# A two-layer fp32 encoder: the first loads of layer 0, two seams of the FFN-out products and the last norm reordered

## The chip, the cores and the metric

The kernel runs on one core of a Trainium2 chip (trn2). The metric is device time in microseconds (us) of one execution. Engines are named as in the profile: PE (TensorE, matmuls), PEld (its weight loads), DVE (VectorE), ACT (ScalarE), POOL (GpSimd), SP (SyncE, which issues most transfers).

## The reference

Input: `x` (1 x 1024 tokens x 1024), `mem` (256 x 1024), positions, and weights for two layers. Cut to what matters, each layer computes

```
h   = rmsnorm(x, g_pre_mix);  z = h @ w_in          # 1024 -> 256 + 512 + 128 + 128 + 256
y_f = fourier(z_f, w_fourier)                        # FFT over tokens and channels, then 64x64 mixes
y_a = window attention(z_q, z_k, z_v, sink)          # 8 query heads, 2 kv heads, window 128, rope
y_m = memory attention(z_m, rmsnorm(mem, g_mem) @ w_mem_kv)
x   = x + rmsnorm(concat(groupnorms of y) @ w_out, g_post_mix)
h   = rmsnorm(x, g_pre_ffn);  gate, up = split(h @ w_ffn_in)   # 1024 -> 2 x 2816
x   = x + rmsnorm((silu(gate) * up) @ w_ffn_out, g_post_ffn)   # 2816 -> 1024
```

all in float32. The output is `x`.

## The kernel before, in words

**Arithmetic.** Every fp32 operand of a large product is held as two fp32r halves: `hi` is a cast (`split`, L176, on ACT) and `lo` is the difference to the original (L177, on DVE, or POOL where `lo_eng` says so). A product is three matmuls per step, hi·hi, hi·lo, lo·hi (`Acc`, L187). `ffn_in` and `ffn_out` are seven half-size products each (a Strassen scheme): `ffn_in` forms sums of weight blocks, `ffn_out` sums of weight blocks and of activations, which were written to DRAM (`actd`) in their seven combinations.

**Memory.** Two arenas in SBUF are handed out by hand: `at(k, ...)` is unit k (256 columns) of the fp32 or the fp32r arena, a `Ring` goes round a list of such places. Weights are first loaded as raw fp32 into the ring `raws` (three places of 512 columns: 0, 2, 4), then split. A buffer's next load waits until the last reader of its former content is done.

**Order.** The program states the work in an order; the tile framework then plans, with a simulated timeline, in which order each engine and each queue runs its instructions, and adds the semaphore waits. `weave` interleaves streams in the program, `tc.issue_after` holds an instruction behind another one. So what stands early in the program can run late and the other way round, but on the chip each engine's queue has a fixed order.

**Start of layer 0 (L1433 to L1444).** `start_load(t)` loads a 512 KB tile of x into place 32 + 4(t mod 5); `start_tile(t)` computes the token's scale from its squares (`token_scale`, L327 to L330), transposes the tile on PE (`norm_T`, L341), and splits it (L176, L177). `mix.zf_load()` (`load_w`, L383) loads the 256 Fourier columns of `w_in` in four transfers, multiplies them with g_pre_mix on POOL (`scaled`, L369), casts on ACT and forms `lo` on POOL. `mix.zf(half)` multiplies them with 512 tokens at a time (`zT`, L187), then the two small `pq` products. `fourier_tables` makes small tables (`w_fourier`, L535; `abp`, L538), `prep` the sine tables on DVE (L283, L288) and ACT. `mem.make()` loads `mem` and `g_mem`, loads `w_mem_kv` (eight transfers of 256 KB, L383), norms and transposes `mem` (`mTp`, L470) and forms keys and values of the memory (`kmp`, `vmp`, L187). Then come tiles 4 to 7 woven with `zf(0)`, and in the loop `zf(1, 2)`, which is the second half in two parts of 256 tokens, and `kvz_load` (`load_w512`, L399, eight transfers through `raws`).

**`ffn_out` (L1342 to L1408).** For each of the seven products i in the order 5, 3, 4, 1, 7, 2, 6 it goes over n = 11 steps k. `out_sums` loads an actd block and one or two `w_ffn_out` blocks, adds or subtracts the latter (L1338, DVE), splits both into a buffer of the ring `abs_` (6 places in layer 0, 15 in layer 1). Then four row parts p take three matmuls each (`step`, L1357), into four PSUM banks `pts`. After the last k each part is evicted (L1380 to L1399). Products 3 and 7 go on accumulating in the banks of 5 and 1: their matmuls of part p wait until part p of the former product has been evicted. In product 6 of the last layer parts 2 and 3 run after parts 0 and 1, each over all k.

**End of layer 1.** `last_tile` calls `residual_out` (L347 to L356) for each finished tile of 128 tokens: squares of the row of f (ACT, L350), their mean and its power -1/2 on POOL (L235, L237), then for each half of 512 columns f·r·g (L354) and x + f (L355), and the store (L356).

Of the kernel before, what the change touches and what calls it, by code (L numbers as in the profile page):

```python
# [12 lines left out]
F32R = mybir.dt.float32r  # L13
I32 = mybir.dt.int32
BF16 = mybir.dt.bfloat16
# [54 lines left out]
def tile_encoder(ctx: ExitStack, tc: tile.TileContext, T, C, out):  # L70
# [169 lines left out]
    def gain(row, g):  # L240
        nc.sync.dma_start(g, row.partition_broadcast(P))
        return g
# [104 lines left out]
    def residual_out(x, f, g, dst, t):  # L347

        ss = sm(1, "rss")
        nc.scalar.activation(junks(D // 2).bitcast(BF16), f, AF.Square, accum_out=ss)  # L350
        r = rsqrt_mean(ss, D, 1, "rrs")
        for n in range(2):
            ns = slice(n * 512, n * 512 + 512)
            nc.vector.scalar_tensor_tensor(out=f[:, ns], in0=f[:, ns], scalar=r[:, 0:1], in1=g[:, ns], op0=ALU.mult, op1=ALU.mult)  # L354
            (nc.gpsimd if t in (1, 3) else nc.vector).tensor_tensor(out=x[:, ns], in0=x[:, ns], in1=f[:, ns], op=ALU.add)  # L355
            (nc.sync, nc.scalar)[n].dma_start(dst[:, ns], x[:, ns])  # L356
# [84 lines left out]
    class Memory:  # L441
# [7 lines left out]
        def load_k(self):  # L449
            self.wk = [load_w(self.w, ci * P, P, self.kw + 8 * ci) for ci in range(2)]  # L450

        def load_v(self):
            self.wv = load_w(self.w, MW, MW, self.kw + 16)

        def rows(self):
            self.h = [at(self.kx + 4 + 4 * mt, D) for mt in range(2)]
            for mt in range(2):
                nc.sync.dma_start(self.h[mt], T["mem"][0, mt * P : (mt + 1) * P, :])

        def norm(self, mt):  # L460
            if mt == 0:
                self.g = gain(T["g_mem"][self.l], at(self.kx, D))
                self.mT = [[at(self.kt + 8 * i + 4 * kg, 4, NMEM, dt=F32R) for kg in range(2)] for i in range(2)]
# [13 lines left out]
        def keys(self, ci):  # L477
            pt = ps([NMEM], "kmp", self.tag)
            acc = Acc(pt, NK)
            for k in range(NK):  # L480
                acc.add(self.wk[ci][k][0], self.wk[ci][k][1], self.m(0, k), self.m(1, k))
            nc.scalar.activation(at(self.ks + ci, NMEM), pt, AF.Copy, scale=QK_SCALE)
# [9 lines left out]
        def make(self):  # L492
            self.rows()
            self.load_k()
# [25 lines left out]
    class Mix:  # L520
# [26 lines left out]
        def zf_load(self):  # L547
            self.wzf = load_w(self.win, 0, 256, 64, nc.gpsimd, self.g)

# [792 lines left out]
    def ffn_out(l, actd, load, out, after, half, late):  # L1342
# [16 lines left out]
        for i in (5, 3, 4, 1, 7, 2, 6):  # L1359
# [5 lines left out]
            for k in range(n):  # L1365
                ops.append(out_sums(l, actd, i, k))
                for p in range(whole):
                    step(pts[p], p, ops[k], k == 0, k == n - 1, new)
# [6 lines left out]
            for p in range(4):  # L1375
                pt = pts[p]
                if p >= whole:
                    for k in range(n):
                        step(pt, p, ops[k], k == 0, k == n - 1, new)
                if i == 5:  # L1380
                    nc.scalar.copy(c22[p], pt)
                    nc.scalar.copy(c11[p], pt)  # L1382
                if i == 3:
                    nc.scalar.copy(c12[p], pt)
                    TT(out=c22[p], in0=pt, in1=c22[p], op=sub)
                if i == 4:
# [45 lines left out]
    mix = Mix(0, hT, mem)  # L1432
    start_load(0)  # L1433
    gains_T(gpT, T["g_pre_mix"], at(15, P))
    for t in range(1, 4):
        start_load(t)
    mix.zf_load()
    start_load(4)
# [4 lines left out]
    mem.make()  # L1443
    weave([lambda t=t: start_tile(t) for t in range(4, 8)], [lambda: mix.zf(0)])  # L1444

    for l in range(DEPTH):
        mix.zf(1, 2)
        mix.kvz_load()
        kvz = mix.skewed(mix.kvz, mix.kvz_turn, NT)
        weave(mix.fourier_units(), kvz[:8] + [mix.q_load] + kvz[8:])  # L1450
# [143 lines left out]
```

## Time and profile before

| | us |
|---|---|
| median of 3 runs (2010.7 to 2011.73) | 2010.85 |
| the profiled execution's own time | 2013.01 |
| its span | 2011.2 |
| PE busy in it | 1967.6 (98%) |
| DVE, ACT, POOL busy | 1489.6, 1047.6, 657.2 |
| transfers: 288.56 MB | 143 GB/s over the span |

The span is the time from the first to the last instruction of the profiled execution. A line of a timeline gives start, length, engine, line, operation, output<-input, and in brackets how long the engine had stood idle before and who released it. A line of the chain of work that ended last gives start, length and what the end waited for. A line of a table by windows gives, for each stretch, the busy time of the engines named with the number of instructions (x), then the granted TensorE clock, the share of the DMA engines and GB/s. Matmuls overlap in their pipe, so a busy PE need not run at its full rate; the number of matmuls in a window shows that better.

### The profile page before, as it was taken

To read this page: it belongs to the slowest core of one execution; us is meant where nothing else is said; L and a number is where in the kernel's file an instruction comes from. 1 tells how busy PE (TensorE), PEld (TensorE's weight loads), DVE (VectorE), ACT (ScalarE), POOL (GpSimd) and SP (SyncE) were. 2 spreads that over 40 slices of the span, in tenths; PEclk is the share of its full clock that TensorE was granted. 3 is DMA by queue.
4 is the path that set the end of the run, shared out by engine and by line. 5 is a ranking of instruction groups with operands and counts; after the bars stand their busy time and mean duration, and the time that the engine had idled before them with its cause. 6 is when DMAs were issued, how large, how long until landed. Compare 5 with 4: busy or idle time off the path is not lost.

```text
span 2011.2 us, 28323 instructions
## 1 busy us (share of the span) xinstructions
PE 1967.6 (98%) x9587; PEld 1628.7 (81%) x9587; DVE 1489.6 (74%) x2364; ACT 1047.6 (52%) x2204; POOL 657.2 (33%) x793
## 2 busy tenths in 40 slices
PE   8999999999999999999999999999999999999998
PEld 7877888788888888887888778877888888887886
DVE  5566867888777766678866677679887777778776
ACT  6476877643433334554555678676343333345541
POOL 4345445204334333002423654451134333400021
PEclk9999999999999999999999999999999999999999
DMA  6210323444323224979831113244332332379973
GB/s 214 64 59 27 110 101 127 135 131 136 100 95 121 85 88 157 310 265 322 286 132 45 53 59 116 95 147 126 126 120 95 121 100 95 110 232 330 314 273 116
DMA packets 181889, 288.56 MB, mean 143 GB/s; under 512 B 15560, under 2 KB 81648, under 8 KB 181744
## 3 DMA queue, kind: packets, MB, share of 16 engines
q1 hardware_dynamic: 173680, 267.88, 40.1%
q10 hardware_dynamic: 8064, 18.88, 2.4%
q8 instruction: 75, 1.23, 0.3%
q14 instruction: 70, 0.57, 0.1%
HBM read 220.11 MB, written 66.58 MB: 143 GB/s over the span
## 4 chain that ended last, share of the span: by engine, by line
PE 87%; DVE 3%; DMA 3%; ACT 2%; issue 2%; POOL 2%; SPq 0%; DVEq 0%; POOLq 0%; ACTq 0%
PE fo L1357 18%; PE qy L1193 12%; PE qx L1193 12%; PE qc L1193 11%; PE mo L187 7%; PE qz L1193 6%; PE kvp L187 4%; PE qp L187 4%; PE zT L187 2%; PE sc L793 2%; PE pT L831 2%; PE qa L1193 1%; PE av L844 1%; DMA arena_f<-in_w_ffn_out 1%; DVE arena_r L177 1%
## 5 line engine op out<-in xcount | busy, mean ns | idle before, releaser
L1357 PE MATMUL fo<-arena_r 128*128 128x512 f32 x1512 | 354.6, 391 | 6.6 <-ACT big L1382 4.0
L1357 PEld LDWEIGHTS fo<-arena_r 128*128 128x128 f32 x1512 | 284.0, 188 | 66.2 <-ACT big L1382 4.8
L176 ACT CAST arena_r<-arena_f 128x512 fp32r<-128x512 f32 (+2 forms) x344 | 185.8, 572 | 179.5 <-DMA arena_f<-actd 69.2
L177 DVE TENSOR_TENSOR arena_r<-arena_f,arena_r 128x512 fp32r<-128x512 f32 x262 | 182.3, 727 | 52.0 <-ACT arena_r L176 44.2
L1193 PE MATMUL qc<-arena_r,flex 128*128 128x512 f32 x912 | 220.8, 390 | 0.0
L1183 ACT CAST flex<-arena_f 128x512 fp32r<-128x512 f32 x148 | 91.8, 621 | 232.2 <-PE qy L1193 71.3
L1193 PEld LDWEIGHTS qc<-arena_r,flex 128*128 128x128 f32 x912 | 171.1, 188 | 37.1 <-DVE flex L1125 0.2
L1193 PE MATMUL qy<-arena_r,flex 128*128 128x512 f32 x576 | 139.4, 389 | 0.0
L1183 ACT CAST arena_r<-arena_f 128x512 fp32r<-128x512 f32 x92 | 57.0, 621 | 156.6 <-DVE arena_f L1180 63.7
L1193 PEld LDWEIGHTS qy<-arena_r,flex 128*128 128x128 f32 x576 | 108.0, 188 | 22.6
L1184 DVE TENSOR_TENSOR flex<-arena_f,flex 128x512 fp32r<-128x512 f32 x148 | 108.4, 734 | 22.7 <-ACT flex L1183 22.7
L1227 POOL TENSOR_TENSOR arena_f<-arena_f 128x512 f32<-128x512 f32 x36 | 48.1, 1336 | 231.7 <-ACT arena_f L1198 231.7
L1193 PE MATMUL qx<-arena_r 128*128 128x512 f32 x360 | 119.5, 389 | 0.0
L1193 PE MATMUL qy<-arena_r 128*128 128x512 f32 x480 | 116.4, 389 | 0.0
L1184 DVE TENSOR_TENSOR arena_r<-arena_f,arena_r 128x512 fp32r<-128x512 f32 x92 | 67.7, 736 | 62.6 <-ACT arena_r L1183 60.5
L1193 PE MATMUL qz<-arena_r,flex 128*128 128x512 f32 x320 | 106.8, 395 | 0.0
L1259 POOL TENSOR_TENSOR arena_f<-arena_f,flex 128x512 f32<-128x512 f32 x28 | 45.7, 1632 | 184.9 <-DVE arena_f L1230 114.1
L1193 PEld LDWEIGHTS qy<-arena_r 128*128 128x128 f32 x480 | 90.1, 188 | 18.7
L1234 POOL TENSOR_TENSOR arena_f<-arena_f 128x512 f32<-128x512 f32 x36 | 60.0, 1668 | 126.5 <-DVE arena_f L1233 126.5
L187 PE MATMUL mo<-big,arena_r 128*128 128x512 f32 x384 | 100.4, 398 | 0.5 <-ACT arena_f L1043 0.5
L1193 PE MATMUL qx<-flex,flex 128*128 128x512 f32 x304 | 100.1, 390 | 0.0
L1180 DVE TENSOR_TENSOR arena_f<-arena_f 128x512 f32<-128x512 f32 x90 | 92.5, 1033 | 4.4 <-DMA arena_f<-in_w_ffn_in 2.9
(315 smaller groups left out, 4624.1 us busy)
## 6 DMA issues: line engine op xcount, KB each, us to landing
arena_f<-in_w_ffn_out SPq DMA_DIRECT2D x264, 256.0 KB, 4.7
actd<-arena_f SPq DMA_DIRECT2D x154, 256.0 KB, 3.0
arena_f<-actd SPq DMA_DIRECT2D x154, 256.0 KB, 4.5
arena_f<-in_w_ffn_in SPq DMA_DIRECT2D x46, 512.0 KB, 3.9
big<-in_w_ffn_in SPq DMA_DIRECT2D x40, 512.0 KB, 4.5
arena_f<-in_w_in SPq DMA_DIRECT2D x40, 256.0 KB, 2.9
arena_f<-in_x SPq DMA_DIRECT2D x16, 512.0 KB, 5.3
arena_f<-in_w_out SPq DMA_DIRECT2D x32, 256.0 KB, 2.7
```

What stands on the lines that cost most here:

```text
L176: nc.scalar.copy(hi, src)
L177: return (lo_eng or nc.vector).tensor_tensor(out=lo, in0=src, in1=f32(hi), op=ALU.subtract)
L187: mm(self.dst, a, b, start=self.i == 0, stop=self.i == self.n - 1)
L793: mm(pt, lhs, self.kst[g][i][:, k0 * P : k1 * P], start=i == 0, stop=i == 1)
L1180: nc.vector.tensor_tensor(out=s, in0=x, in1=y, op=op)
L1183: self.cast = nc.scalar.copy(w[:, 0], s)
L1184: self.lo = nc.vector.tensor_tensor(out=w[:, 1], in0=s, in1=f32(w[:, 0]), op=ALU.subtract)
L1193: mm(pt, a, b, start=start and n == 0, stop=n == 11, skip_group_check=not start)
L1227: G(out=self.u2, in0=self.u2, in1=self.p1, op=ALU.add)
L1234: G(out=self.p5, in0=self.p1, in1=self.p5, op=ALU.add)
L1259: (G if i % 2 else nc.vector).tensor_tensor(out=q.act[i], in0=c, in1=g[i], op=ALU.mult)
L1357: mm(pt, ab[:, 0, x, sl], ab[:, 1, y], start=new and first and j == 0, stop=last and j == 2, skip_group_check=not new)
```

## The change

Five things differ.

- `residual_out`: the squares are taken for each half of 512 columns by itself, f is multiplied with g before the scale r is known, and r comes in with the addition of x. POOL adds the mean of the first half's squares to the second's.
- `Memory`: the 256 key columns are loaded as one block of weights (rows of 256 columns) in place of two blocks of 128; the gain row is loaded with the rows of `mem`; in layer 0 these three loads stand ahead of `start_load(4)`.
- Start of layer 0: order x0, gains, x1, `w_in`, x2, x3, `mem`, x4. `raws` has seven places until `kvz_load` has been stated, then again three. Two of the new places (44, 46) lie in tile 3's place of x.
- `zf_load` in layer 0: POOL writes `hi` (raw times gain, rounded) and DVE forms `lo` (raw times gain minus hi), 256 columns at a time, in place of POOL, ACT and POOL. `zf(0)` runs in two parts of 256 tokens.
- `ffn_out`: in products 5 and 1 the last three steps k are run part by part: all three for part 0, then for part 1, and so on, each part's eviction behind it. Product 5 is copied from PSUM once and not twice, and product 3's subtraction reads that copy.

```diff
     def residual_out(x, f, g, dst, t):
-        ss = sm(1, "rss")
-        nc.scalar.activation(junks(D // 2).bitcast(BF16), f, AF.Square, accum_out=ss)
-        r = rsqrt_mean(ss, D, 1, "rrs")
-        for n in range(2):
-            ns = slice(n * 512, n * 512 + 512)
-            nc.vector.scalar_tensor_tensor(out=f[:, ns], in0=f[:, ns], scalar=r[:, 0:1], in1=g[:, ns], op0=ALU.mult, op1=ALU.mult)
-            (nc.gpsimd if t in (1, 3) else nc.vector).tensor_tensor(out=x[:, ns], in0=x[:, ns], in1=f[:, ns], op=ALU.add)
+        ss, v, r = (sm(2, "rss2"), sm(2, "rrsv2"), sm(1, "rrs"))
+        cols = [slice(n * 512, n * 512 + 512) for n in range(2)]
+        for n, ns in enumerate(cols):
+            nc.scalar.activation(junks(256).bitcast(BF16), f[:, ns], AF.Square, accum_out=ss[:, n : n + 1])
+            nc.gpsimd.tensor_scalar(
+                out=v[:, n : n + 1], in0=ss[:, n : n + 1], scalar1=1.0 / D, scalar2=v[:, 0:1] if n else EPS, op0=ALU.mult, op1=ALU.add
+            )
+            nc.vector.tensor_tensor(out=f[:, ns], in0=f[:, ns], in1=g[:, ns], op=ALU.mult)
+        nc.gpsimd.tensor_tensor(out=r, in0=v[:, 1:2], in1=mhalf[:, 0:1], op=ALU.pow)
+        for n, ns in enumerate(cols):
+            nc.vector.scalar_tensor_tensor(out=x[:, ns], in0=f[:, ns], scalar=r[:, 0:1], in1=x[:, ns], op0=ALU.mult, op1=ALU.add)
             (nc.sync, nc.scalar)[n].dma_start(dst[:, ns], x[:, ns])
...
         def load_k(self):
-            self.wk = [load_w(self.w, ci * P, P, self.kw + 8 * ci) for ci in range(2)]
+            self.wk = load_w(self.w, 0, MW, self.kw)
...
         def rows(self):
+            self.g = gain(T["g_mem"][self.l], at(self.kx, D))
             self.h = [at(self.kx + 4 + 4 * mt, D) for mt in range(2)]
...
         def make(self):
-            self.rows()
+            if self.l:
+                self.rows()
             self.load_k()
...
         def zf_load(self):
-            self.wzf = load_w(self.win, 0, 256, 64, nc.gpsimd, self.g)
+            if self.l:
+                self.wzf = load_w(self.win, 0, 256, 64, nc.gpsimd, self.g)
+                return
+            self.wzf = []
+            for k0 in (0, 4):
+                hi, lo = at(64 + 2 * k0, 4, 256, dt=F32R), at(68 + 2 * k0, 4, 256, dt=F32R)
+                for j in (0, 2):
+                    raw = raws(2, 256)
+                    r0 = (k0 + j) * P
+                    nc.sync.dma_start(raw, self.win[r0 : r0 + 2 * P, 0:256].rearrange("(k p) c -> p k c", p=P))
+                    for i in range(2):
+                        g = self.g[:, k0 + j + i : k0 + j + i + 1]
+                        h = hi[:, j + i]
+                        nc.gpsimd.tensor_scalar(out=h, in0=raw[:, i], scalar1=g, scalar2=1.0, op0=ALU.mult, op1=ALU.mult)
+                        nc.vector.scalar_tensor_tensor(
+                            out=lo[:, j + i], in0=raw[:, i], scalar=g, in1=f32(h), op0=ALU.mult, op1=ALU.subtract
+                        )
+                self.wzf += [(hi[:, i], lo[:, i]) for i in range(4)]
...
             for k in range(n):
                 ops.append(out_sums(l, actd, i, k))
-                for p in range(whole):
+                for p in range(whole if i not in (5, 1) or k < n - 3 else 0):
                     step(pts[p], p, ops[k], k == 0, k == n - 1, new)
...
             for p in range(4):
                 pt = pts[p]
-                if p >= whole:
-                    for k in range(n):
-                        step(pt, p, ops[k], k == 0, k == n - 1, new)
+                for k in range(0 if p >= whole else n - 3 if i in (5, 1) else n, n):
+                    step(pt, p, ops[k], k == 0, k == n - 1, new)
                 if i == 5:
-                    nc.scalar.copy(c22[p], pt)
                     nc.scalar.copy(c11[p], pt)
                 if i == 3:
                     nc.scalar.copy(c12[p], pt)
-                    TT(out=c22[p], in0=pt, in1=c22[p], op=sub)
+                    TT(out=c22[p], in0=pt, in1=c11[p], op=sub)
...
     start_load(0)
+    raws.ks = (0, 2, 4, 52, 54, 44, 46)
     gains_T(gpT, T["g_pre_mix"], at(15, P))
-    for t in range(1, 4):
+    start_load(1)
+    mix.zf_load()
+    for t in range(2, 4):
         start_load(t)
-    mix.zf_load()
+    mem.rows()
     start_load(4)
...
-    weave([lambda t=t: start_tile(t) for t in range(4, 8)], [lambda: mix.zf(0)])
+    weave([lambda t=t: start_tile(t) for t in range(4, 8)], [lambda: mix.zf(0, 2)])
...
         mix.kvz_load()
+        raws.ks, raws.i = (0, 2, 4), 0
```

More of the change, by code (lines that the diff above doesn't have):

```diff
@@ L461, in norm @@
             if mt == 0:
-                self.g = gain(T["g_mem"][self.l], at(self.kx, D))
                 self.mT = [[at(self.kt + 8 * i + 4 * kg, 4, NMEM, dt=F32R) for kg in range(2)] for i in range(2)]
@@ L479, in keys @@
             acc = Acc(pt, NK)
+            cs = slice(ci * P, ci * P + P)
             for k in range(NK):
-                acc.add(self.wk[ci][k][0], self.wk[ci][k][1], self.m(0, k), self.m(1, k))
+                acc.add(self.wk[k][0][:, cs], self.wk[k][1][:, cs], self.m(0, k), self.m(1, k))
             nc.scalar.activation(at(self.ks + ci, NMEM), pt, AF.Copy, scale=QK_SCALE)
```

## The prediction

> **What bounds the kernel now.** I read the page first, then the chain of waits in order of time for the start, then tables by windows, and last the timelines of the places that the change touches.
>
> ```profile
> PE 1967.6 (98%) x9587; PEld 1628.7 (81%) x9587; DVE 1489.6 (74%) x2364; ACT 1047.6 (52%) x2204; POOL 657.2 (33%) x793
> ```
>
> PE is the bound over the whole span: of 2011.2 us only 43.6 are idle. The change removes no product, so it can gain only what PE loses: idle time, and time in which it is busy below its rate. The chain shows such time at the start, in four transfers on which the end hung:
>
> ```profile
> 6.03 6.67 DMA arena_f<-in_w_fourier
> ...
> 29.65 2.86 DMA arena_f<-in_w_mem_kv
> ...
> 36.85 3.68 DMA arena_f<-in_w_mem_kv
> ...
> 48.26 2.65 DMA arena_f<-in_w_in
> ...
> 57.16 3.12 PE zT L187 x24
> ```
>
> What PE lost there, and why the transfers were late, is in the waits of PE and of SP's queue:
>
> ```profile
> PE zT L187 <- ACT flex L176: 3.6, 1, 3.6
> PE abp L538 <- DMA arena_f<-in_w_fourier: 2.7, 1, 2.7
> ```
>
> ```profile
> SPq L383 <- DMA arena_f<-in_w_mem_kv: 6.9, 2, 5.5
> SPq L383 <- DVE flex L288: 5.1, 2, 4.9
> ```
>
> SP held loads of L383, `w_mem_kv` and a `w_in`, back for 6.9 + 5.1 = 12.0 us, because with three raw places a load needs an old one's last reader, and that sits on DVE behind the sine work (L288). Two windows show the price on PE:
>
> ```profile
> 10.00:15.00 5.00, 2.33 (x12) 2.20 (x12) 2.52 (x5) 4.70 (x12) 4.53 (x10) 1.00 1.00 331
> ...
> 50.00:55.00 5.00, 1.35 (x11) 1.11 (x10) 1.54 (x3) 3.65 (x8) 4.50 (x5) 0.92 0.65 206
> 55.00:60.00 5.00, 5.00 (x34) 5.00 (x33) 2.90 (x4) 3.15 (x6) 1.35 (x2) 0.74 0.28 90
> ```
>
> After the idle at 50 to 55 the granted clock is 0.74. The second place is `ffn_out` (matmuls of L1357 alone; PE's count is the first x):
>
> ```profile
> 820.00:830.00 10.00, 9.54 (x42) 7.57 (x42) 1.00 0.90 320
> 920.00:930.00 10.00, 9.59 (x43) 7.60 (x41) 1.00 0.84 273
> 930.00:940.00 10.00, 7.43 (x32) 5.93 (x32) 1.00 0.97 350
> 1810.00:1820.00 10.00, 6.59 (x30) 5.11 (x28) 0.94 0.99 340
> 1820.00:1830.00 10.00, 9.91 (x32) 7.96 (x33) 0.72 0.96 335
> 1830.00:1840.00 10.00, 10.00 (x46) 8.29 (x45) 1.00 1.02 368
> ```
>
> 46 in 10 us (0.217 us each) is the full rate. At 1810 to 1830, where product 5 ends and 3 begins in layer 1, 30 of 92 are missing, in part from a clock of 0.72 after the gap. Layer 0 misses 4 at the same seam (820 to 830) and 3 + 14 where 1 passes into 7 (920 to 940).
>
> **The change part by part: the tail.** After the last matmul everything is serial:
>
> ```profile
> 2002.56 0.69 DVE L1397 TENSOR_TENSOR big<-fo,big 128x512 f32<-128x512 f32 x1 [1.98 <-PE fo L1357]
> 2003.35 1.06 ACT L350 ACTIVATE arena_f<-big 128x1024 bf16<-128x1024 f32 x1 [6.33 <-DVE big L1397]
> ...
> 2004.58 0.19 POOL L235 TENSOR_SCALAR rrsv<-rss 128x1 f32<-128x1 f32 x1 [6.65 <-ACT arena_f L350]
> 2004.86 0.55 POOL L237 TENSOR_TENSOR rrs<-rrsv,const 128x1 f32<-128x1 f32 x1
> 2005.44 1.42 DVE L354 SCALAR_TENSOR_TENSOR big<-big,rrs,flex 128x512 f32<-128x512 f32 x2 [2.19 <-POOL rrs L237]
> 2006.77 1.29 DVE L355 TENSOR_TENSOR arena_f<-arena_f,big 128x512 f32<-128x512 f32 x2
> 2008.09 0.34 ACTq L356 DMA_DIRECT2D out<-arena_f  x1
> ```
>
> The left half of f is finished by product 2, so its squares and its product with g lie beside product 6. Behind the last eviction ACT squares 512 columns and not 1024: about half of 1.06, a gain of 0.5 (estimate). The multiplication with g runs on DVE while ACT and POOL work (2003.3 to 2005.4, DVE idle 2.19), so of the four DVE operations after the power two are left: from 2005.44 to 2008.06 was 2.62, two take 1.42, a gain of 1.2. The store behind it stays. Sum 1.7; bounds 1.2 (the square saves nothing) and 2.0. For tiles 1 and 3 the addition moves from POOL to DVE, two operations of 0.65 per tile, beside products in which PE is bound: nothing.
>
> **The seams.** The row parts of product 3 wait for the evictions of product 5. In layer 1 these stood in ACT's queue behind casts that waited for DVE and a transfer:
>
> ```profile
> 1818.45 0.62 ACT L176 CAST arena_r<-arena_f 128x512 fp32r<-128x512 f32 x1 [1.07 <-DVE arena_f L1338]
> ...
> 1819.45 0.59 ACT L1382 COPY big<-fo 128x512 f32<-128x512 f32 x1
> ...
> 1820.09 1.65 PE L1357 MATMUL fo<-arena_r 128*128 128x512 f32 x3 [3.50 <-ACT big L1382]
> ```
>
> Run part by part, the last three steps are 9 matmuls per part, so part 0 is finished 27 x 0.217 = 5.9 us before the product's end, part 1 3.9, part 2 2.0, and each needs one copy, not two. The copy of part 0 then has 5.9 us and more, where the gap was 3.50. The price: the operands of the last step are needed when part 0 reaches it, 30 matmuls (6.5 us) before the end and not 12 (2.6): 3.9 us earlier.
>
> ```profile
> 1807.58 0.62 ACT L176 CAST arena_r<-arena_f 128x512 fp32r<-128x512 f32 x1 [0.42 <-DMA arena_f<-actd]
> 1808.23 0.69 DVE L177 TENSOR_TENSOR arena_r<-arena_f,arena_r 128x512 fp32r<-128x512 f32 x1
> ...
> 1813.71 2.88 PE L1357 MATMUL fo<-arena_r 128*128 128x512 f32 x12
> ```
>
> The last step began at 1813.71; its operands, if I read the ring rightly, were there at 1808.92, 4.8 us earlier. So 0.9 us of margin is left. I take 5.5 of the 30 x 0.217 = 6.5 us; part 3's copy is still at the very end and may cost the rest. Bounds 2.5 (operands 3.9 late) to 6.5. At layer 0's seam of 5 the gain is at most 4 x 0.217 = 0.9; I take 0.5. At its seam of 1:
>
> ```profile
> 931.75 0.68 DVE L1390 TENSOR_TENSOR big<-fo,big 128x512 f32<-128x512 f32 x1
> ...
> 932.57 1.61 PE L1357 MATMUL fo<-arena_r 128*128 128x512 f32 x6 [2.60 <-ACT arena_r L176]
> ```
>
> Eviction (till 932.43) and cast end together: DVE and ACT are late with both. The change spreads the evictions but DVE's work stays; I take 1.0, from -3.9 (operands needed earlier) to 17 x 0.217 = 3.7. Seams together 7.0. That three of the six places of layer 0's ring are held to the end costs nothing as long as the other three feed product 3 for its first 3 x 2.6 us.
>
> **The start.** Of the transfers in the chain the last three are held by `raws`; four more places let them start with the tiles of x. Upper end: 2.86 + 3.68 + 2.65 = 9.2, and the 2.7 of `abp`, 11.9; the idle 3.6 at 54 is the third one's effect and not counted again. Lower end: `mem`, `g_mem` and the fourth `w_in` load, 1.75 MB, may now stand in SP's queue ahead of `w_fourier`; at 331 GB/s (last column, 10 to 15) that delays `abp`, and the tiles queued behind it on PE, by 5.3: -5.3.
>
> Which is nearer? What comes next is ACT: 4.70 of 5 us busy at 10 to 15, 3.65 and 3.15 at 50 to 60. It loses the four casts of `w_in` but must do all others in a shorter time. I take half of the upper end, 6. The weights of `zf` now go through POOL and DVE:
>
> ```profile
> L369 POOL TENSOR_SCALAR arena_f<-arena_f,const 128x256 f32<-128x256 f32 x8 | 3.7, 483 | 0.1
> ...
> L288 DVE SCALAR_TENSOR_TENSOR flex<-flex 128x256 f32<-128x256 f32 x10 | 4.6, 458 | 0.1
> ...
> 44.57 1.46 DVE L407 SCALAR_TENSOR_TENSOR big<-arena_f,const,big 128x512 fp32r<-128x512 f32 x1 [0.26 <-ACT big L406]
> ...
> 47.48 0.75 DVE L407 SCALAR_TENSOR_TENSOR big<-arena_f,const,big 128x512 fp32r<-128x512 f32 x1 [0.32 <-ACT big L406]
> ```
>
> Eight steps of 0.483 and a last 0.458 are 4.3 us from first to last. But L407, the same operation at twice the width, took 1.46 beside a POOL operation and 0.75 alone. Doubled on both engines the chain takes 8.2; the 3.9 come off the start's gain at most. [...] `zf(0)` in halves lets its first part start with two tiles; it costs 96 narrow matmuls at 3.12/24 = 0.130 for 48 wide ones at 3.02/12 = 0.252: 0.4.
>
> ```profile
> 31.20 3.02 PE L187 MATMUL zT<-arena_r 128*128 128x512 f32 x12
> ```
>
> The key weights in one block and the order of their rows move the same bytes by as many instructions: nothing.
>
> **Sum.** 1.7 + 7.0 + 6 - 0.4 = 14.3. The profiled execution took 2013.01 (span 2011.2 and 1.8 around it), 2.2 above the median of the runs; the differences come off the median: 2010.85 - 14.3 = 1996.5.
>
> **The rivals.** (1) The start gains little: POOL and DVE hold each other up as above, and ACT's fixed order keeps what transfers no longer hold. For it: ACT's 4.70 of 5. Start 1.5 and not 6: 2001.
> (2) The seams don't do what the text says: the planner may mix the part order again, or the operands come just in time, so that PE waits before the end what it no longer waits after it. For it: the margin of 0.9. Seams 1 and not 7: 2002.5.
> (3) All of it: start 11.9, seams 6.5 + 0.9 + 3.7: 2010.85 - 1.7 - 11.9 + 0.4 - 11.1 = 1986.5.
> (4) Slower: the need for operands 3.9 us earlier decides. Wherever the last step's operands are ready less than 6.5 us before the product's end, PE stands 3.9 and then runs at 0.72 for 10 us (2.8): 6.7. At all four seams 26.8, against 6.5 + 0.9 + 3.7 lost now: 15.7 more. With the start and the tail 2010.85 + 15.7 - 7.3 = 2019. Against it: 15 places in layer 1, and the margin.
>
> **How the numbers follow.** Forecast 0.50, rival (1) 0.22, (2) 0.12, (3) 0.08, (4) 0.08. A measurement can tell about 0.2% (4 us) from no change: faster means below 2006.8. Rivals (1) and (2) together (start 1.5, seams 1) would give 2007, and the start's lower end in place of the 6 2007.8; I put 0.10 on no change. The range reaches from rival (3) over (1) and (2) to that edge: 1987 to 2007. Faster 0.83, same 0.10, slower 0.07.
>
> **What would show it.** The tail: about 7 us, not 8.7, from the last matmul to the end of the span, with two DVE operations after the power. The seam of layer 1: no gap above 1 us, 44 or more matmuls of L1357 in each 10 us, granted clock 1.00. The start: `w_mem_kv` transfers gone from the chain, SP's waits on L383 below 5 us, `zf`'s second half some 6 us earlier. Wrong if a new gap stands inside the last three steps of products 5 or 1, if `abp` waits longer than 2.7 us, or if PE loses time in stages that the change doesn't touch.

## The result, and the profile after

| | us |
|---|---|
| before, median of 6 runs (2007.76 to 2015.37) | 2011.07 |
| after, median of 6 runs (1995.89 to 2003.06) | 1998.99 |
| after : before, 95% interval | 0.994 (0.9924 to 0.9956) |
| after once more, on another chip, median of 6 runs | 1998.57 |
| its ratio | 0.9926 (0.9899 to 0.9953) |
| profiled execution of after: own time, span | 1995.89, 1994.1 |

The change makes the kernel 12.1 us faster (8.8 to 15.3 by the interval); the forecast was 14.3. The two profiled executions lie 17.1 us apart, more than the medians: the one before was 1.9 above its median, the one after 3.1 below.

The first line of the page of after (busy time, share of the span, instructions):

```profile
PE 1961.6 (98%) x9635; PEld 1625.0 (81%) x9635; DVE 1493.8 (75%) x2378; ACT 1043.0 (52%) x2210; POOL 650.5 (33%) x793
```

PE idles 32.5 us of 1994.1, where it was 43.6 of 2011.2; its busy time is 6.0 less although it runs 48 matmuls more. That is the time in which it was busy below its rate.

**Where the 17.1 us went.** The first column gives a point of the program, by the start of the first or the end of the last matmul of the named output in each trace; the last column what was gained since the point above.

| | before | after | gained |
|---|---|---|---|
| layer 0: end of the last `kvp` | 124.24 | 119.74 | 4.5 |
| first `fo` | 795.58 | 790.96 | 0.1 |
| last `fo` | 1026.69 | 1019.43 | 2.65 |
| layer 1: first `qp` | 1109.63 | 1102.38 | 0.0 |
| last `qp` | 1181.02 | 1171.35 | 2.4 |
| first `fo` | 1786.50 | 1776.89 | -0.1 |
| end of the last `fo` | 2002.52 | 1986.50 | 6.4 |
| end of the span | 2011.22 | 1994.11 | 1.1 |

Four of these are places of the change: the start, the two `ffn_out`, the tail. Nothing was forecast for layer 1's key and query stage, where 2.4 were gained; it comes up at the end.

**The seams.** Table by windows of after, its `fo` matmuls (L1380) alone; columns as before: us, PE and PEld busy (x), granted clock, DMA share, GB/s:

```profile
820.00:830.00 10.00, 10.00 (x46) 8.29 (x45) 1.00 0.83 283
920.00:930.00 10.00, 9.65 (x42) 7.39 (x41) 1.00 1.01 360
930.00:940.00 10.00, 9.80 (x44) 7.80 (x43) 1.00 0.89 290
...
1810.00:1820.00 10.00, 10.00 (x46) 8.29 (x45) 1.00 1.01 353
1820.00:1830.00 10.00, 10.00 (x46) 8.29 (x45) 1.00 1.02 366
```

All 46 are there at the seams of product 5; in layer 1 the windows that held 30 and 32 hold 46 at a clock of 1.00. Where 1 passes into 7, 86 stand in two windows, before 75.

**The start.** The three longest waits of PE in the first 70 us of after, without the 4.6 us for the gains (`ggp`) that both kernels have, then one of SP's queue there:

```profile
PE zT L187 <- DVE arena_r L177: 1.6, 1, 1.6
PE zT L187 <- ACT arena_r L176: 1.3, 2, 0.9
PE hTp L341 <- ACT arena_f L495: 1.0, 1, 1.0
```

```profile
SPq L387 <- DVE flex L177: 3.8, 3, 3.2
```

The waits for `w_fourier` (2.7) and for the cast of late weights (3.6) are gone. SP's longest wait on L387 (before L383) is 3.8 us, where the two longest were 12.0 together. With all smaller waits of this line it is 5.6 us, and it was 17.1. Table by windows of after, whole core (PE, PEld, DVE, ACT, POOL busy):

```profile
30.00:35.00 5.00, 3.16 (x23) 2.51 (x22) 5.00 (x13) 4.49 (x11) 2.33 (x4) 1.00 0.68 211
35.00:40.00 5.00, 5.00 (x44) 5.00 (x43) 4.96 (x10) 3.60 (x6) 1.31 (x3) 1.00 0.63 178
40.00:45.00 5.00, 5.00 (x44) 5.00 (x44) 4.93 (x6) 2.77 (x7) 4.82 (x4) 1.00 0.34 103
45.00:50.00 5.00, 4.03 (x34) 3.79 (x34) 4.11 (x7) 2.74 (x6) 2.59 (x5) 1.00 0.00 0
50.00:55.00 5.00, 4.27 (x33) 3.73 (x33) 2.69 (x5) 4.06 (x8) 0.53 (x3) 1.00 0.26 105
```

The hole of before (50 to 55, 1.35 us busy) has become three shallow ones, and in these windows the clock stays at 1.00. No transfer stands in the chain between 26 and 60 us any more; it runs through DVE, which is busy 14.89 of 15 us from 30 to 45.

**The tail.** Timeline of after, from the last eviction on:

```profile
1986.54 0.69 DVE L1418 TENSOR_TENSOR big<-fo,big 128x512 f32<-128x512 f32 x1 [2.63 <-PE fo L1380]
1987.32 0.63 ACT L352 ACTIVATE arena_f<-big 128x512 bf16<-128x512 f32 x1 [6.00 <-DVE big L1418]
...
1988.08 0.69 DVE L356 TENSOR_TENSOR big<-big,flex 128x512 f32<-128x512 f32 x1 [0.85 <-ACT arena_f L352]
1988.22 0.68 POOL L353 TENSOR_SCALAR rrsv<-rss,rrsv 128x1 f32<-128x1 f32 x1 [4.92 <-ACT arena_f L352]
1988.98 0.55 POOL L357 TENSOR_TENSOR rrs<-rrsv,const 128x1 f32<-128x1 f32 x1
1989.57 1.42 DVE L359 SCALAR_TENSOR_TENSOR arena_f<-big,rrs,arena_f 128x512 f32<-128x512 f32 x2 [0.80 <-POOL rrs L357]
```

From the last matmul to the end it is 7.61 us and not 8.70. The square took 0.63 for 1.06, and two operations follow the power. But POOL's step on one column took 0.68 where its like took 0.19 before: it began 0.14 us after DVE's product of two SBUF operands, which had waited for ACT, because it overwrites the f that ACT reads.

### The profile page after: what moved, and what is told of

It is laid out like the page before. It is cut to its first block, busy times and chain, and to the rows that moved or that the text cites. A ratio compares the mean times of both kernels' runs of the same rounds, so it can differ in the third digit from the quotient of the medians.

```text
span 1994.1 us, 28456 instructions
## 1 busy us (share of the span) xinstructions
PE 1961.6 (98%) x9635; PEld 1625.0 (81%) x9635; DVE 1493.8 (75%) x2378; ACT 1043.0 (52%) x2210; POOL 650.5 (33%) x793
## 4 chain that ended last, share of the span: by engine, by line
PE 88%; DVE 3%; ACT 2%; POOL 2%; issue 2%; DMA 1%; DVEq 0%; POOLq 0%; SPq 0%; ACTq 0%
PE fo L1380 19%; PE qx L1216 12%; PE qy L1216 12%; PE qc L1216 11%; PE mo L187 7%; PE qz L1216 6%; PE kvp L187 4%; PE qp L187 4%; PE sc L816 2%; PE zT L187 2%; PE pT L854 2%; PE qa L1216 1%; PE av L867 1%; DMA arena_f<-in_w_in 1%; PE ms L935 1%
## 5 line engine op out<-in xcount | busy, mean ns | idle before, releaser
L1380 PE MATMUL fo<-arena_r 128*128 128x512 f32 x1512 | 354.0, 390 | 0.6 <-DVE arena_r L177 0.5
L1380 PEld LDWEIGHTS fo<-arena_r 128*128 128x128 f32 x1512 | 283.1, 188 | 59.9 <-DVE arena_r L177 0.9
L177 DVE TENSOR_TENSOR arena_r<-arena_f,arena_r 128x512 fp32r<-128x512 f32 x262 | 178.2, 714 | 42.6 <-ACT arena_r L176 32.5
L1216 PE MATMUL qx<-arena_r 128*128 128x512 f32 x360 | 119.5, 389 | 0.0
L1207 DVE TENSOR_TENSOR arena_r<-arena_f,arena_r 128x512 fp32r<-128x512 f32 x92 | 66.7, 725 | 62.3 <-ACT arena_r L1206 60.2
L1361 DVE TENSOR_TENSOR arena_f<-arena_f 128x512 f32<-128x512 f32 x110 | 81.2, 743 | 20.7 <-DMA arena_f<-in_w_ffn_out 19.9
```

The lines of the kernel that those rows point to most:

```text
L177: return (lo_eng or nc.vector).tensor_tensor(out=lo, in0=src, in1=f32(hi), op=ALU.subtract)
L1207: self.lo = nc.vector.tensor_tensor(out=w[:, 1], in0=s, in1=f32(w[:, 0]), op=ALU.subtract)
L1216: mm(pt, a, b, start=start and n == 0, stop=n == 11, skip_group_check=not start)
L1361: nc.vector.tensor_tensor(out=s, in0=x, in1=y, op=op)
L1380: mm(pt, ab[:, 0, x, sl], ab[:, 1, y], start=new and first and j == 0, stop=last and j == 2, skip_group_check=not new)
```

## The experiments

My theory: each of the three parts gains by itself, the seams by the order of the steps (not by the copy that is saved), the start by places and order of the loads together, until DVE is the bound. Rivals: the saved copy frees ACT and that is all; the raw places alone are the start's gain; ACT bounds the start.

**The tail alone.** The edit is the change's `residual_out` and nothing else.

```diff
     def residual_out(x, f, g, dst, t):
-        nc.scalar.activation(junks(D // 2).bitcast(BF16), f, AF.Square, accum_out=ss)
...
+        for n, ns in enumerate(cols):
+            nc.scalar.activation(junks(256).bitcast(BF16), f[:, ns], AF.Square, accum_out=ss[:, n : n + 1])
...
```

> The kernel before with the new residual_out alone. Theory (the three parts act each at its own place): from the last matmul to the end of the span 7.6 us and not 8.7, as in the changed kernel, and nothing else; the time falls by 1.1 us, 0.05%, which timing can hardly tell. The POOL step behind the last squares takes 0.68 and not 0.19, because DVE multiplies f by g beside it. Rival (the tail gains the 1.7 forecast, and the 0.68 is chance): 7.0 us from the last matmul to the end.

Measured: 2009.46 (12 runs), ratio 0.9992 (0.998 to 1.0004). From the last matmul to the end 7.59 us; POOL's step 0.68 again. The tail's gain is 1.1 us, and no time of the whole kernel could show it.

**The seams alone**: the change's edits in `ffn_out`.

```diff
-                for p in range(whole):
+                for p in range(whole if i not in (5, 1) or k < n - 3 else 0):
...
+                for k in range(0 if p >= whole else n - 3 if i in (5, 1) else n, n):
...
-                    nc.scalar.copy(c22[p], pt)
...
-                    TT(out=c22[p], in0=pt, in1=c22[p], op=sub)
+                    TT(out=c22[p], in0=pt, in1=c11[p], op=sub)
```

> The kernel before with the part-by-part order of the last three steps in products 5 and 1 and the single copy. Theory: about 9 us faster (6.4 at the seam of layer 1, 2.7 in layer 0), 0.45%; no gap over 1 us at the layer 1 seam and clock 1.00 there. Rival (the gain of the changed kernel there came from an earlier start, which shifted transfers against the seam): under 4 us.

Measured: 2005.55 (12 runs), ratio 0.997 (0.9959 to 0.9981), 6.0 us (3.8 to 8.2), less than the 9 expected from the two profiles. All 46 matmuls stand in each window at 820, 1810 and 1820, and PE waits at none of the seams of product 5.

**One copy, old order**: of these edits the last three lines.

```diff
-                    nc.scalar.copy(c22[p], pt)
...
-                    TT(out=c22[p], in0=pt, in1=c22[p], op=sub)
+                    TT(out=c22[p], in0=pt, in1=c11[p], op=sub)
```

> The kernel before with product 5 copied from PSUM once and not twice, the order of the steps as before. Theory (the copies stand behind casts that wait, and only the order lets them out earlier): the gap at the layer 1 seam shrinks by the 0.5 us of one copy, to about 3.0; gain below 2 us, or up to 4 if the shorter gap no longer brings the clock down. Rival (ACT's load is the cause, the order only decoration): most of the 6.4 us.

Measured: 2011.32 (12 runs), ratio 0.9993 (0.9981 to 1.0004). Timeline of PE at layer 1's seam:

```profile
1814.24 2.88 PE L1357 MATMUL fo<-arena_r 128*128 128x512 f32 x12
1818.69 0.96 PE L1357 MATMUL fo<-arena_r 128*128 128x512 f32 x3 [1.57 <-ACT big L1381]
```

The gap is still there, 1.57 us for 3.50; about 3.0 was expected. After it the clock stayed at 1.00 here, and layer 1's `ffn_out` took 211.5 us, where the six kernels with the old order and two copies took 214.1 to 216.0. So in this one profile the single copy gained 3 us at the seam, but the time of the kernel shows no gain clear of the noise.

**New order, two copies**: the rest of the edits.

```diff
-                for p in range(whole):
+                for p in range(whole if i not in (5, 1) or k < n - 3 else 0):
...
+                for k in range(0 if p >= whole else n - 3 if i in (5, 1) else n, n):
```

> The kernel before with the part-by-part order of the last three steps in products 5 and 1, and product 5 still copied from PSUM twice. Theory (the order is the cause, the single copy an extra of under 1 us): 5 to 6.5 us faster, no gap over 1 us at the layer 1 seam. Rival (both are needed, since two copies per part, 1.2 us, stand between casts that wait): under 3 us and a gap of 1 us or more.

Measured: 2004.53 (5 runs), ratio 0.9966 (0.9953 to 0.9979), 6.8 us. Its windows, `fo` matmuls alone:

```profile
1810.00:1820.00 10.00, 10.00 (x45) 8.03 (x44) 1.00 1.00 355
1820.00:1830.00 10.00, 10.00 (x46) 8.29 (x45) 1.00 0.98 332
```

So the order alone brings the seams' gain; with it, the second copy costs nothing that can be seen. The rival, that the saved copy is all, falls. That the copy by itself can shorten the gap stays: the two edits work on the same gap, and their gains don't add up.

**The start alone**: every edit outside `residual_out` and `ffn_out`.

```diff
     start_load(0)
+    raws.ks = (0, 2, 4, 52, 54, 44, 46)
...
+    start_load(1)
+    mix.zf_load()
...
+    mem.rows()
     start_load(4)
...
```

> The kernel before with all edits of the start and the memory block, seams and tail as before. Theory: layer 0's first FFN-out matmul comes 4.6 us earlier, as in the changed kernel, and the time falls by 4 to 5 us, 0.2%. Rival (the gain in layer 1's key and query stage, 2.4 us in the profile of the changed kernel, belongs to the memory block or to the ring's new phase): that stage is 2.4 us shorter here too, and the time falls by 7.

Measured: 2006.07 (12 runs), ratio 0.9973 (0.9961 to 0.9986), 5.4 us (2.8 to 7.8). Layer 1's key and query stage took 69.1 us here (before 71.4), as the rival had it, but the time fell by 5.4 and not by 7. The three parts alone sum to 1.6 + 6.0 + 5.4 = 13.0 us, whole 12.1 and 14.9: within their intervals they add up. Then the start was taken apart.

**Only the seven raw places:**

```diff
     start_load(0)
+    raws.ks = (0, 2, 4, 52, 54, 44, 46)
...
+        raws.ks, raws.i = (0, 2, 4), 0
```

> The kernel before with seven places for raw weights until the key and value weights are loaded, all else as before. Theory (the held-back transfers were the loss at the start, as the prediction put it): 3 to 5 us faster, the first FFN-out matmul of layer 0 some 4 us earlier, the memory weights' transfers gone from the chain. Rival (DVE, busy 5.00 of 5 us from 30 to 45 in the changed kernel, is the next bound, so that transfers alone gain little): under 2 us.

Measured: 2015.16 (12 runs), ratio 1.0024 (1.0014 to 1.0034): slower, where 3 to 5 us of gain were expected.

**The whole start, but three raw places:**

```diff
     start_load(0)
-    raws.ks = (0, 2, 4, 52, 54, 44, 46)
```

The line that sets the ring back to its first place behind `kvz_load` stays.

> All edits of the start and the memory block, but three raw places as before. Theory (the places are the cause): 0 to 2 us faster than the kernel before, against 6 with seven places. Rival (order, two-tile products and the POOL and DVE weights gain by themselves): 4 us or more.

Measured: 2017.06 (12 runs), ratio 1.0024 (1.0013 to 1.0035): slower as well.

**The start, but the first `w_in` weights by POOL, ACT and POOL as before:**

```diff
     def zf_load(self):
-            if self.l:
-                self.wzf = load_w(self.win, 0, 256, 64, nc.gpsimd, self.g)
-                return
...
+            self.wzf = load_w(self.win, 0, 256, 64, nc.gpsimd, self.g)
```

> All edits of the start and the memory block, but the first w_in weights made as before, by POOL, ACT and POOL. Theory (places and order are the cause; POOL and DVE hold each other up in the new way, so it gains little): within 1.5 us of the 6 that all edits gain. Rival (the weights' chain is what the first product waits for): 3 us or less, and the first zT matmul at 12 us or later, not at 9.

Measured: 2009.6 (11 runs), ratio 0.9996 (0.9985 to 1.0006): no difference to before. The first `zT` stands at 10.42 us, in the start alone at 8.93.

All three kernels with a part of the start miss its gain, and with it what was expected. At the start itself they don't: the last `kvp` of layer 0 ends earlier in each. They lose it between there and the first `fo` of layer 0, in code that no edit touches, and a good part of it at 360 to 390 us. Timeline of PE there, first of the kernel before, then of the one with seven raw places:

```profile
364.02 1.06 PE L1118 MATMUL hTp<-const,arena_f 128*128 128x128 f32 x8 [1.22 <-DVE arena_f L321]
...
370.84 2.88 PE L1193 MATMUL qc<-arena_r,flex 128*128 128x512 f32 x12
374.25 0.73 PE L1193 MATMUL qa<-arena_r,flex 128*128 128x512 f32 x2 [0.53 <-ACT flex L1183]
```

```profile
372.64 1.04 PE L1118 MATMUL hTp<-const,arena_f 128*128 128x128 f32 x8
373.43 2.99 PE L1193 MATMUL qc<-arena_r,flex 128*128 128x512 f32 x12
379.06 0.96 PE L1193 MATMUL qa<-arena_r,flex 128*128 128x512 f32 x2 [2.64 <-ACT flex L1183]
```

The order of the instructions differs. Before, eight transposes `hTp` stand ahead of the last 24 matmuls of `mo`, which run while their result is split; here they stand behind them, and PE waits 2.64 us for ACT. The window behind this wait, whole core:

```profile
380.00:390.00 10.00, 10.00 (x44) 8.30 (x43) 8.46 (x12) 4.05 (x8) 1.16 (x3) 0.86 0.33 113
```

In this stretch every kernel of the study has one of the two orders, A (as before) or B. The table gives each one's end of the last `kvp` of layer 0, the time from there to its first `fo`, and the lengths of the two `ffn_out` (first to last `fo`):

| kernel | last `kvp` | order | to first `fo` | `ffn_out` 0 | `ffn_out` 1 |
|---|---|---|---|---|---|
| before | 124.2 | A | 671.3 | 231.1 | 216.0 |
| tail alone | 124.9 | A | 672.9 | 231.5 | 214.1 |
| seams alone | 123.4 | A | 672.9 | 227.7 | 209.6 |
| one copy, old order | 125.7 | A | 672.8 | 230.5 | 211.5 |
| new order, two copies | 125.5 | A | 672.8 | 228.7 | 209.8 |
| start alone | 120.1 | A | 671.8 | 231.9 | 214.4 |
| only seven raw places | 122.9 | B | 678.1 | 229.5 | 214.2 |
| start, three raw places | 122.0 | B | 677.8 | 233.6 | 215.1 |
| start, old weights | 120.2 | B | 676.3 | 233.6 | 214.3 |
| after | 119.7 | A | 671.2 | 228.5 | 209.6 |
| after once more | 117.4 | A | 671.8 | 233.1 | 209.6 |
| after, own place for f*g | 119.5 | A | 673.3 | 228.3 | 209.7 |
| after, preparation late | 123.7 | B | 676.3 | 230.5 | 209.6 |
| after, both | 124.1 | B | 674.1 | 228.0 | 209.8 |

The nine kernels of order A take 671.2 to 673.3 us (mean 672.3) from `kvp` to `fo`, the five of order B 674.1 to 678.1 (mean 676.5): 4.2 us, a little less than what the start gains.

The wait above is not the whole of it. Counted from the last `kvp`, at points where PE has run the same matmuls in both orders, order B is behind by 1.0 us on the mean at 258 us of the kernel before, by 3.0 at 325, by 2.5 at 373, just ahead of this wait, and by 4.2 at the first `fo`. In the kernel with three places the wait is 1.13 us, and all of its loss stands earlier.

By its own rows, each kernel gains at the start (the five kernels with the old start have a mean of 124.8) and loses against order A's mean: places alone 1.9 and 5.8, three places 2.8 and 5.5, old weights 4.6 and 4.0. Measured were 4.8 us slower, 4.8 slower and 0.8 faster. The signs fit; 1 us of the first and 2 of the second stay unexplained, and two profiles of one kernel (after, and after once more) differ by 2.3 us at the last `kvp`. That the order is the cause is read from this table: no run turned the order alone.

**The changed kernel once more**, beside three variants on one chip:

> The changed kernel once more, beside three variants of it on the same chip. If what was seen between the two profiles belongs to the change, its ratio to the kernel before is again about 0.994 (0.9925 to 0.9955), the first zT matmul stands near 9.8 us, the first FFN-out matmul of layer 0 near 791 us (4 to 5 us ahead of the kernel before), 46 matmuls in every 10 us of 1800 to 1830, and the granted clock is 1.00 there. The key/query stage of layer 1 is the open point: both kernels waited 1.7 us there, the one before at a granted clock of 0.66 afterwards, the changed one at 1.00. If that difference is chance, the 2.4 us that the changed kernel gained in this stage can be missing here; if it belongs to the change it is there again.

Measured: 1998.57 (6 runs), ratio 0.9926 (0.9899 to 0.9953). First `zT` at 8.74, last `kvp` 2.3 us earlier again, 46 matmuls in each window at layer 1's seam. The key and query stage of layer 1 again took 69.0 us (before 71.4). In this execution `ffn_out` of layer 0 had two waits of 1.4 us at 1008 to 1012, one of them behind a late `actd` transfer, and took 233.1.

**A place of its own for f*g of the right half:**

```diff
-            nc.vector.tensor_tensor(out=f[:, ns], in0=f[:, ns], in1=g[:, ns], op=ALU.mult)
+            fg.append(at(4, 512) if n else f[:, ns])
+            nc.vector.tensor_tensor(out=fg[n], in0=f[:, ns], in1=g[:, ns], op=ALU.mult)
...
-            nc.vector.scalar_tensor_tensor(out=x[:, ns], in0=f[:, ns], scalar=r[:, 0:1], in1=x[:, ns], op0=ALU.mult, op1=ALU.add)
+            nc.vector.scalar_tensor_tensor(out=x[:, ns], in0=fg[n], scalar=r[:, 0:1], in1=x[:, ns], op0=ALU.mult, op1=ALU.add)
```

> The changed kernel, with the right half of f*g in the last residual written to a buffer of its own, so that VectorE needn't wait for ScalarE to have read f. Theory: at the end of the changed kernel GpSimd's one-column step took 0.68 us instead of 0.19 only because VectorE's product of two SBUF operands (0.69 us, started 0.14 us before it) ran beside it. Then VectorE's product starts beside the ScalarE square instead, it is over when GpSimd begins, the step is back at 0.19 us, and from the last matmul to the end 7.6 us become about 7.1 us: some 0.5 us, ratio to the changed kernel 0.9997, far under what a time can tell; the profile rows decide. Rival: the step is slow because its second scalar operand is a column of SBUF instead of a constant. Then it stays at 0.68 us and the tail stays at 7.6 us.

Measured: 1999.59 (7 runs), ratio to before 0.9933 (0.991 to 0.9956); against the changed kernel no difference. Timeline of its tail:

```profile
1990.47 0.69 DVE L358 TENSOR_TENSOR arena_f<-big,flex 128x512 f32<-128x512 f32 x1
1990.53 0.63 ACT L353 ACTIVATE arena_f<-big 128x512 bf16<-128x512 f32 x1 [6.00 <-DVE big L1420]
...
1991.43 0.27 POOL L354 TENSOR_SCALAR rrsv<-rss,rrsv 128x1 f32<-128x1 f32 x1 [6.12 <-ACT arena_f L353]
1991.78 0.55 POOL L359 TENSOR_TENSOR rrs<-rrsv,const 128x1 f32<-128x1 f32 x1
```

With DVE's product over before POOL begins, the step takes 0.27 us, and the tail 7.17 for 7.61. The theory holds, the rival (the column operand) is left with 0.08 us.

**The preparation of the tables behind the second tiles:**

```diff
     mix.fourier_tables(58)
-    prep()
     mem.make()
     weave([lambda t=t: start_tile(t) for t in range(4, 8)], [lambda: mix.zf(0, 2)])
+    prep()
```

> The changed kernel, with the preparation of the norm gains and of the sine and cosine tables of the positions moved behind the second half of the first token tiles: the same instructions, later in each engine's order. Theory: the start of the changed kernel is bound by VectorE, busy 5.00, 4.96 and 4.93 of 5 us between 30 and 45 us, some 4 to 5 us of it this preparation; moved behind, the first kvp matmuls start 2 to 4 us earlier, VectorE shows gaps between 30 and 45 us, and the span falls by 2 to 4 us (ratio to the changed kernel 0.998 to 0.999) if the later stages keep their order. Rival: the bound at the start is the arrival of the weights or ScalarE; then the milestones of the first 100 us move by under 1 us and the time stays, or is 2 to 4 us longer when the preparation is waited for behind it. A second rival: the start gains and it is given back in the out stage, at 130 to 400 us, where another order of the PE's groups leaves waits of 1.5 to 2.6 us, as in the runs with a part of the start edits.

Measured: 2004.73 (12 runs), ratio to before 0.9962 (0.9946 to 0.9977): some 6 us slower than the changed kernel on that chip. A window of it, whole core, then a wait of PE:

```profile
45.00:50.00 5.00, 5.00 (x45) 4.93 (x43) 0.69 (x1) 2.29 (x6) 1.48 (x2) 1.00 0.21 84
```

```profile
PE kT L768 <- POOL arena_f L734: 2.9, 1, 2.9
```

The first half of the theory holds: DVE is relieved (0.69 of 5 us, in the changed kernel 4.11), and PE is busy 28.03 and not 26.46 of the 30 us from 30 to 60. At 79 us PE has run the same matmuls 0.6 us earlier than in the changed kernel, of 2 to 4 expected. But at 92 us it is 4.0 behind: its key transposes wait 2.9 us for POOL, and the granted clock of the next 5 us (90 to 95) is 0.74 (0.87 from 90 to 100). Timeline of POOL in the changed kernel, then of POOL and of DVE in this one:

```profile
49.40 0.61 POOL L727 TENSOR_SCALAR st<-const 128x64 f32<-128x64 f32 x2 [2.41 <-DVE const L308]
```

```profile
79.53 7.47 POOL L727 TENSOR_SCALAR st<-const 128x64 f32<-128x64 f32 x2 [9.64 <-DVE const L308]
```

```profile
79.34 0.68 DVE L606 TENSOR_TENSOR flex<-arena_f 128x512 f32<-128x512 f32 x1
79.94 1.29 DVE L606 TENSOR_TENSOR arena_f<-arena_f 128x512 f32<-128x512 f32 x2
...
85.10 1.43 DVE L606 TENSOR_TENSOR flex<-arena_f 128x256 f32<-128x256 f32 x4
86.56 0.86 DVE L442 TENSOR_TENSOR arena_r<-zT,arena_r 64x256 fp32r<-64x256 f32 x2
89.20 0.53 DVE L731 TENSOR_TENSOR arena_f<-arena_f,const 128x128 f32<-128x128 f32 x1 [1.78 <-POOL arena_f L734]
```

POOL scales the first finished table columns (L727): two steps, 0.61 us in the changed kernel at 49 us, 7.47 us here. The first step alone took 7.19 of them, the second 0.31 as elsewhere. From 79.34 to 86.53 DVE ran 18 operations of two SBUF operands without a pause, most of them Fourier sums (L606). POOL's first step was over at 86.71, 0.18 us after the last of them. So by these rows what the moved work cost is not the preparation's length but where its end falls: in a run of DVE of 7.2 us, beside which POOL's pair took 7.47 us and not 0.61. No run moved this step alone. With that the last `kvp` ends at 123.7, and the order is B. The rivals that the preparation is waited for and that the order turns came true together; my reason for neither was this one.

**Both edits:**

> The two edits together on the changed kernel. Theory: they add up, the start by 2 to 4 us and the tail by 0.5 us, ratio to the kernel before about 0.992. Rival: nothing or slower, by the reasons given for the late preparation alone; then the tail's rows still show GpSimd's step at 0.19 us.

Measured: 2003.68 (12 runs), ratio to before 0.996 (0.9945 to 0.9976); tail 7.18, last `kvp` 124.1, order B, and POOL's pair takes 7.47 us again. The edits don't add up to a gain, and no version here has a better time than the changed kernel.

## Why the prediction was right, point by point

14.3 us were forecast and 12.1 (8.8 to 15.3) measured. The parts' errors went both ways: by the profiles the tail gained 0.6 less and the seams 0.6 more than forecast.

**The tail (1.7): right in kind, 0.6 too high.** The square gained 0.43, DVE's two operations less 1.2. What the step missed is that "the multiplication with g runs on DVE while ACT and POOL work" held for ACT no longer: in place, it waits for ACT's read, and then POOL's step runs beside it at 0.68 for 0.19.

**The seams (7.0): right.** Layer 1: the kernels with the old order and two copies have a mean of 214.7 us, those with the new order 209.7: 5.0, forecast 5.5. The 216.0 of the profile I read is the longest of the six old ones: its gap was 3.50 us (the others 2.69 to 3.59), and the clock behind it fell to 0.50 in a window of 5 us. It fell in four of the other five too, to 0.66 to 0.82. Layer 0: means of 231.9 and 229.3, gain 2.6, forecast 1.5; here the rows overlap (229.5 to 233.6, and 227.7 to 233.1). Together 7.6; by times 6.0 (3.8 to 8.2). The operands came in time: no wait before the end of product 5 in any profile with the new order, so rival (4) and the gap inside the last three steps did not come. At layer 0's seam of product 1 PE still waits up to 1.0 us in some of these profiles. That each part "needs one copy, not two" was not needed for the gain.

**The start (6, less 0.4): the size right, the reason half wrong.** The last `kvp` ends at a mean of 119.2 us in the four profiles with the whole start in order A (117.4 to 120.1), against 124.8 (123.4 to 125.7): 5.6. But I put it down to the four places alone. By one profile each, which can be off by 2 us, the places alone gain 1.9 and the other edits with three places 2.8; it takes both for the 5.6. "What comes next is ACT" failed for the most part: the chain runs through DVE, with the sine work in the midst of splits, and the late preparation, which took 8.1 us of work off DVE and 0.6 off ACT between 30 and 60 us, got PE 1.6 us. But ACT isn't out of it: of PE's own waits in the first 70 us of after, ACT ended 3.9 us and DVE 2.4. Of DVE's operations between 25 and 50 us in after (busy us, mean ns):

```profile
L288 DVE SCALAR_TENSOR_TENSOR flex<-flex 128x256 f32<-128x256 f32 x10 | 6.7, 667 | 0.2
L411 DVE SCALAR_TENSOR_TENSOR big<-arena_f,const,big 128x512 fp32r<-128x512 f32 x4 | 4.4, 1093 | 0.0
```

L288 took 667 ns on the mean, 458 before. The signs said for the start came in part: the memory's weights are gone from the chain and `abp` doesn't wait; SP's waits on L387 are 5.6 in all, not below 5; and the chain's 24 `zT` matmuls moved from 57.16 to 52.94, 4.2 us earlier and not 6.

**The new weights for `zf`: my lower price holds.** By group of after, POOL and then DVE:

```profile
L567 POOL TENSOR_SCALAR arena_r<-arena_f,const 128x256 fp32r<-128x256 f32 x8 | 3.9, 492 | 2.0 <-DMA arena_f<-in_w_in 1.9
```

```profile
L568 DVE SCALAR_TENSOR_TENSOR arena_r<-arena_f,const,arena_r 128x256 fp32r<-128x256 f32 x8 | 4.2, 565 | 1.9 <-POOL arena_r L567 1.9
```

0.492 and 0.565 for 0.483 and 0.458: nearly a quarter more on DVE, no doubling. (Doubled on both engines the chain would have been 8.6 us; my 8.2 doubled POOL's steps only. And the L407 of 0.75 us was not "alone": it kept its length beside POOL's L704, whose step took 0.87 us there for 0.32.) Here DVE waits for POOL's half and POOL for the transfer, so that they overlap in part only; the price that I set against the start was paid by L288 instead, 2.1 us in ten operations, most of it beside POOL's splits at 44 to 47 us. That POOL and DVE hold each other up, as rival (1) has it, shows at L288 (667 ns for 458) and hardly at these weights. With the old weights the last `kvp` ends at 120.2, with the new ones at 120.1: as far as one profile each tells, this piece does nothing at the start.

**"PE loses time in stages that the change doesn't touch"** I named as a sign of error. It did not happen to this change, but to every second variant: the plan's order at 340 us. That the changed kernel keeps order A is the step that I had not looked at, and it is worth nearly as much as the start: as far as the prediction goes, this was luck. Which property of the start tips the order is open: neither the places nor the weights alone decide, since the kernels without the one and without the other both have B.

**The 2.4 us in layer 1's key and query stage** are two things. Two waits of PE in before, then the one that is left in after:

```profile
PE kT L745 <- POOL arena_f L711: 0.9, 1, 0.9
PE qp L187 <- DVE big L407: 1.7, 1, 1.7
```

```profile
PE qp L187 <- DVE big L411: 1.7, 1, 1.7
```

The first wait, 0.9 us, comes with the start: it is 0.7 to 1.4 us in the six kernels that lack the start's new order and memory block, and at most 0.2 in the eight that have them. Why, no run shows. The second, 1.7 us for DVE's weights, stands in all 14 profiles. Windows of before, after, and after with a place of its own for f*g, at this wait and behind it:

```profile
1120.00:1125.00 5.00, 3.26 (x19) 2.37 (x17) 3.56 (x6) 4.92 (x13) 2.81 (x3) 1.00 0.31 104
1125.00:1130.00 5.00, 5.00 (x18) 4.04 (x19) 3.22 (x6) 1.73 (x5) 3.42 (x7) 0.66 0.19 65
```

```profile
1115.00:1120.00 5.00, 3.27 (x18) 2.69 (x18) 4.29 (x8) 3.16 (x11) 2.61 (x7) 1.00 0.32 105
1120.00:1125.00 5.00, 5.00 (x24) 4.11 (x23) 4.59 (x10) 4.65 (x12) 3.24 (x5) 1.00 0.02 5
```

```profile
1115.00:1120.00 5.00, 3.26 (x12) 2.23 (x11) 4.20 (x7) 3.98 (x11) 3.20 (x5) 0.88 0.41 124
1120.00:1125.00 5.00, 5.00 (x22) 3.99 (x22) 3.40 (x6) 2.56 (x6) 3.13 (x6) 0.78 0.11 39
```

About the same 1.73 us of idle is followed by a lower clock in 6 of the 14 profiles (the stage then takes 70.4 to 71.9 us) and by 1.00 in 8 (68.8 to 70.2). The lower clock came in four of those six and in two of those eight. So few profiles can't tell whether the change has a part in these 1.5 us or whether it is chance. It is one of the reasons why a single profile of after looked 5 us better than the medians.

## What to carry to other kernels

Where accumulators pass from one product to the next, finish them one part after the other: spreading the last few steps hid the evictions of product 5 (5.0 us at layer 1's seam), and a copy saved on top of it was worth nothing more. With a planner that orders the queues, an edit at the start is also a new draw for stages far behind; compare the instruction order and the length of the untouched stages before you judge a part of a change by its time. When the bound moves, ask beside what the pushed work will then run: taking the tables off DVE's busiest stretch gave PE 1.6 us, and their end in the wrong place took 4.6.

## What the runs showed of the hardware that was not expected

- **POOL beside DVE's two-operand work.** At the tail a one-column step took 0.68 us beside DVE's product of two SBUF operands and 0.27 when that was over. A step of 128x64 took 0.31 us at one place and, with the late preparation, 7.19 beside an unbroken run of 18 such operations of 0.28 to 0.69 us; the pair that it belongs to took 0.61 us in the changed kernel and 7.47 in both kernels with the late preparation. At the tail and in that run DVE's operation had begun first, 0.14 and 0.19 us ahead of POOL's step; DVE's products of 128x512 took 0.69 us beside POOL's step and 0.69 with POOL idle, and POOL ended 0.13 and 0.18 us after the last of DVE's operations. Beside POOL's splits at 44 to 47 us of the changed kernel DVE was slowed as well (L288 up to 1.40 us; at 38.0 us, with POOL idle, it took 0.42). By what the two hold each other up, no run shows.
- **The clock after short waits.** About 1.73 us of idle was followed by a lower granted clock in 6 of 14 profiles, 0.66 in the worst window of 5 us, and by 1.00 in the other 8. What decides between the two, no run shows.
